# Data operations moved off GpSimd, and the modulation's accumulation ordered behind diag(1/rms), in a two-layer RWKV-7 / Hyena block on one core

## The chip, the cores and the metric

The kernel runs on one core of one Trainium2 chip. The metric is device time in microseconds (us): the median of 3 runs was 3515.73 (3511.09 to 3516.47). One further execution was taken by the hardware profiler; all rows shown are from it.

The engines are named as in the profile: PE (TensorE matmul), PEld (its weight load), DVE (VectorE), ACT (ScalarE), POOL (GpSimd), SP (SyncE, which here only issues DMAs). Each engine works through its own instructions in the order in which they stand, and waits on semaphores for the others. A DMA is issued by an instruction in the queue of SP or of POOL; if that instruction has to wait, what stands behind it in that queue waits too.

## The reference, cut to what matters

Two layers on a latent stream x of 256 tokens x 2048 channels, with a context of 256 tokens as prefix in the first layer. Layer 0 mixes tokens with a bidirectional RWKV-7 scan, layer 1 with a Hyena long convolution; each mixer is followed by a squared-ReLU MLP of width 8192.

```python
for i in range(DEPTH):                              # 2 layers
    mod = (silu_c @ ada_w[i] + ada_b[i]).reshape(B, N_MOD, 1, D)     # 2048 x 12288 per layer
    h = modulate(rms_norm(x, norm_g[i, 0]), mod[:, 0], mod[:, 1])
    y = rwkv_mixer(...) if kind == 0 else hyena_stream(h, ...)
    x = x + mod[:, 2] * rms_norm(y, norm_g[i, 1])
    h = modulate(rms_norm(x, norm_g[i, 2]), mod[:, 3], mod[:, 4])
    x = x + mod[:, 5] * rms_norm(squared_relu_mlp(h, mlp_up[i], mlp_down[i]), norm_g[i, 3])
```

Two parts of it matter here. The first is `mod`, the modulation: one row vector silu(c), 2048 long, times a 2048 x 12288 matrix per layer. It is a matrix-vector product, whose 100 MB of weights per layer have to be fetched. The second is `x + gate * rms_norm(y)`, the residual at the end of each of the four sublayers, with the next sublayer's norm right behind it.

In the mixer of layer 0, the decay and the in-context rate are sigmoids of low-rank products (two directions each, 2048 channels x 512 tokens), and the scan is done in chunks, for which triangular 32x32 systems are inverted.

## The kernel before, in words

**Stages.** In the order of time of the profiled execution: norms and modulation of layer 0 (to about 200 us); the RWKV projections (200 to 440); the beginning of the scan, in which the low-rank products and the first chunks overlap (440 to 520); the scan in groups of heads (520 to 1280); the Hyena filters and the rest of the scan (to 1386); the RWKV output gemm (1386 to 1470); first transition T1 (1470 to 1530); MLP of layer 0, `mlp0` (1530 to 2240); second transition T2 (2240 to 2285); Hyena's input gemm and convolutions (2285 to 2650); Hyena's output gemm (2650 to 2744); third transition T3 (2744 to 2797); MLP of layer 1, `mlp1` (2797 to 3495); the last residual. The transition's numbers run from the last matmul of a gemm to the first sublayer matmuls that run without a break.

**Gemms.** Each fp32 weight block `w` (128 x 1024, loaded by SP) is cut by ACT into a high part `wh` and by DVE into a low part `wl`, and three matmuls per block (`hxh,wh`; `hxl,wh`; `hxh,wl`) make the product. In mlp0 and mlp1 these keep PE busy without a pause.

**A transition** is `resid` (from L443) with `rstd` in it. The token-major outputs (tiles `o` or `y`) are squared by ACT with a row sum (`ysq`), DVE sums the four quarters into `ss`, ACT takes the square root, DVE the reciprocal, and two DVE instructions write `dg`, a 128x128 diagonal matrix of 1/rms for each half of the tokens (L463). Only then can PE go on: `sg` matmuls (L469) transpose the output and scale it in one product with `dg`. For each of 16 channel blocks DVE then makes x (residual), ACT the high part `hxh` of the next input and the squares `sq`, DVE the low part `hxl`, and PE the sums of squares (L423) and the next gemm's matmuls. When all 16 are there, `rstd` is computed (ACT square root, DVE reciprocal) and the first products of the next gemm are scaled by it (`nt` in an MLP, `z` in Hyena).

**The modulation** of what is needed later is computed beside other stages by `ada_run`, which is a generator: the surrounding code advances it by a step now and then (`bg`, `rate`). It works on sets: one set is 512 columns of `ada_w`. For a set, 16 blocks of 128 rows are loaded into tiles `aw`, two blocks per load (`per=2`, 512 KB) or one (`per=1`, 256 KB), in two buffers, and for each block DVE adds the block, scaled by a column `sc` of silu(c), to the sum `acc` (128x512): a TENSOR_SCALAR for the first block (L332), 15 SCALAR_TENSOR_TENSOR for the others (L334). Four small matmuls with a column of ones then sum over the partitions (L313). `ADA = (4, 8, 16, 8, 4)` gives the number of sets in the RWKV projections, the scan (there in another way, by PE), mlp0, Hyena and mlp1. A load into `aw` has to wait until the acc step that read this buffer is done. The loads of mlp0's sets (128 x 512 KB) and of the RWKV projections (64 x 256 KB) are in SP's queue, between the loads of the weights; those of Hyena (128 x 256 KB) and of mlp1 (32 x 512 KB) are in POOL's queue.

**What sets the order.** The instructions are emitted in program order into a scheduler that places them by a simulated time line and by priorities; `high_priority` (around `ss` to `dg`) draws instructions forward. The order on each engine is then fixed in the program, and so an acc step that stands ahead of the chain to `dg` on DVE is waited for, even where its load is late.

**POOL** does four other things: 32 of the 64 instructions t*0.5+0.5 behind the tanh of the low-rank products in `lora2` (L750, tile `l2t`; the other 32 are on DVE); in `scan_prepare`, for each of 8 groups, the memset of the 128x1024 tile W of the triangular inversion and of its diagonal (L1303 and L1304, printed as tile `d`); the memset of the two edge columns of each of 48 tiles `z` in Hyena (L1581); and the issue of the loads `fx` of the scan's projections (L857) with the stores `xv` and `xr` behind which they stand.

Of the kernel before, what the change touches and what calls it, by code (L numbers as in the profile page):

```python
# [10 lines left out]
F32 = mybir.dt.float32  # L11
F32R = mybir.dt.float32r
BF16 = mybir.dt.bfloat16
AF = mybir.ActivationFunctionType
# [4 lines left out]
P = 128  # L19
D = 2048  # L20
KT = D // P
L = 256
# [47 lines left out]
class Kern:  # L70
    def __init__(self, nc, tc, I, out, scr, upto=99):
        nc = Nc(self, nc)
        self.nc, self.tc, self.I, self.out, self.scr = nc, tc, I, out, scr
        self.bg, self.credit, self.rate = [], 0.0, 0.0
        self.upto = upto
        self.wraw, self.wsp = [], []

# [22 lines left out]
    def pin(self, key, r):  # L100

        if self.pins is not None and key in self.pinned:
            prev = self.pins.get(key)
            if prev is not None:
                self.tc.add_manual_dep(r.ins, prev.name, mybir.DependencyInfo(mybir.DependencyClass.NoSync, mybir.DependencyReason.DATA),
                                       reason="order of the scan")
            self.pins[key] = r.ins
        return r

# [130 lines left out]
    def setup(self, es):  # L240
# [17 lines left out]
        nc.vector.memset(self.ones, 1.0)  # L258
        self.eps = cst.tile([P, 2], F32, name="eps")
# [45 lines left out]
    def ada_run(self, n, pool, psum="mm", on_pool=True, per=2, bufs=2, behind=None, queue=None):  # L305
# [12 lines left out]
        for layer, ch, i in itertools.islice(self.ada_todo, n):  # L318
            acc = pool.tile([P, 512], F32, name="acc", bufs=per)
            c0 = ch * D + i * 512  # L320
            for k in range(0, KT, per):
# [3 lines left out]
                for a in range(per):  # L325
# [5 lines left out]
                    elif k + a == 0:  # L331
                        nc.vector.tensor_scalar(acc, w[:, a], s, None, op0=ALU.mult)  # L332
                    else:
                        nc.vector.scalar_tensor_tensor(acc, w[:, a], s, acc, op0=ALU.mult, op1=ALU.add)  # L334
# [108 lines left out]
    def resid(self, x, y, ss, layer, gi, ch, pool, nxt=None):  # L443
# [13 lines left out]
        with self.tc.high_priority(self.PRT):  # L457
# [4 lines left out]
            for tt in range(2):  # L462
                nc.vector.tensor_scalar(dg[:, tt], self.ident, ss[:, 1, tt : tt + 1], None, op0=ALU.mult)  # L463
# [242 lines left out]
    def lora2(self, pool):  # L706
# [33 lines left out]
        for q in range(4):  # L740
            for nm, e in (("dec", 0), ("dec", 1), ("a", 0), ("a", 1)):
                b0 = self.hw0 if nm == "dec" else self.ha0
                w = next(block)
                for j in range(4):
# [5 lines left out]
                    (nc.gpsimd if m % 4 < self.LPOOL else nc.vector).tensor_scalar(t, t, 0.5, 0.5, op0=ALU.mult, op1=ALU.add)  # L750
# [521 lines left out]
    def scan_prepare(self, g):  # L1272
# [30 lines left out]
        nc.gpsimd.memset(W, 0.0)  # L1303
        nc.gpsimd.memset(fl(W)[:, 0:1024:33], 1.0)  # L1304
# [251 lines left out]
    LPOOL = 2  # L1556
# [3 lines left out]
    def hyena(self, x, ada, nada):  # L1560
        nc, tc, I = self.nc, self.tc, self.I
        with ExitStack() as es:
# [7 lines left out]
            fp = pool("hf", 4)  # L1570
            r = self.xr
            ys = []
            self.bg, self.rate = [itertools.islice(ada, nada // 4)], nada / 4 / 11
            for dc in range(4):
                secs = []
                for s in range(3):
                    zc = [None] * 4

                    def ev(m, ps, s=s, zc=zc):
                        z = zp.tile([P, L + 2], F32, name="z", bufs=2)  # L1580
                        nc.gpsimd.memset(z[:, 0 : L + 2 : L + 1], 0.0)  # L1581
# [173 lines left out]
    def run(self):  # L1755
        nc, tc = self.nc, self.tc
        with ExitStack() as es:
# [28 lines left out]
            with ExitStack() as e1:  # L1786
# [7 lines left out]
                for i, phase in enumerate((lambda: self.mlp(x, 0), lambda: self.hyena(x, (), 0), lambda: self.mlp(x, 1))):  # L1794
                    if self.upto >= 3 + i:
                        with ExitStack() as e2:
                            if self.ADA[2 + i]:
                                ad = self.pool(e2, "ad")
                                per = 1 if i == 1 else 2
                                ada = self.ada_run(self.ADA[2 + i], ad, "sg", self.ONP[2 + i], per, queue=nc.gpsimd if i else None)  # L1800
# [98 lines left out]
```

## Time and profile before

The profiled execution took 3515.95 us, of which the trace's span covers 3513.1; 2.85 us lie around it. The profiled execution is 0.22 us above the median of the runs shown.

| | before |
|---|---|
| median of 3 runs | 3515.73 us (3511.09 to 3516.47) |
| profiled execution | 3515.95 us, span 3513.1 us |
| PE busy | 3290.9 us (94%) |
| DVE busy | 2474.5 us (70%) |
| ACT busy | 1638.0 us (47%) |
| POOL busy | 253.4 us (7%), 476 instructions |
| mean granted TensorE clock | 0.974 |

PE is the engine to read first: it works during 94% of the span, so a change can gain at most in the pauses of PE and in the stretches where its clock is low. A stage in which PE is busy all the time is not shortened by moving DVE's or POOL's work; a transition is, if what moves was in the chain that PE waits for.

### The profile page before, as it was taken

The page shows a single profiled execution, that of the slowest core. Times are in us where ns is not written, and L with a number is a line of the kernel's source. Part 1 is how long each engine was busy: PE and PEld are TensorE (multiplying, and loading weights), DVE is VectorE, ACT ScalarE, POOL GpSimd, SP SyncE. Part 2 cuts the span into 40 slices and gives each one's busy share as a digit, 9 for nine tenths or more (in the row PEclk, how much of TensorE's full clock was granted, in tenths as well). Part 3 has the DMA queues.
Part 4 walks back from the last instruction along what each step waited for, and adds up shares of the span by engine and source line. Part 5 has one row for each costly group of instructions (what it writes and reads, how often), then busy time and mean ns, then how long its engine had stood idle before and what let it go on. Part 6 is the DMA issues. An engine that isn't in the chain of part 4 may idle for free.

```text
span 3513.1 us, 74240 instructions
## 1 busy us (share of the span) xinstructions
PE 3290.9 (94%) x30598; PEld 2886.2 (82%) x30598; DVE 2474.5 (70%) x4059; ACT 1638.0 (47%) x2878; POOL 253.4 (7%) x476
## 2 busy tenths in 40 slices
PE   6799888989999888899999999999999899999999
PEld 3377677878888766798989899899997798989897
DVE  4798776767777755587777876588997875555554
ACT  4554454555444444444444444454453444444453
POOL 0011121111111000000000001011110100000000
PEclk9999999999999989999999999999999999999999
DMA  9668899989889745688888886477775775555653
GB/s 313 204 227 278 277 330 283 289 267 272 269 267 277 219 140 182 202 260 285 277 299 279 297 282 236 142 250 238 240 231 185 242 243 188 183 189 187 188 189 120
DMA packets 575515, 836.76 MB, mean 238 GB/s; under 512 B 39551, under 2 KB 373280, under 8 KB 575176
## 3 DMA queue, kind: packets, MB, share of 16 engines
q1 hardware_dynamic: 529224, 668.42, 59.3%
q0 software_dynamic: 45952, 163.60, 14.7%
q8 instruction: 239, 3.92, 0.5%
q14 instruction: 100, 0.82, 0.1%
HBM read 777.31 MB, written 54.59 MB: 237 GB/s over the span
## 4 chain that ended last, share of the span: by engine, by line
PE 60%; DMA 11%; DVE 8%; issue 5%; ACT 2%; SPq 1%; POOL 0%; DVEq 0%; POOLq 0%; ACTq 0%
PE mm L112 47%; DMA aw<-in_ada_w 4%; PE sg L112 4%; PE fl L112 4%; PE sc L112 3%; DVE tmp L53 1%; DVE d L53 1%; DVE wl L53 1%; DMA cum<-cum 1%; DMA fx<-xv 1%; DMA w<-in_hy_in_w 1%; DVE acc L53 1%; DMA win<-in_window 1%; DMA fr<-in_w_v 1%; PE sg L469 1%
## 5 line engine op out<-in xcount | busy, mean ns | idle before, releaser
L53 DVE TENSOR_TENSOR wl<-w,wh 128x1024 fp32r<-128x1024 f32 (+1 forms) x716 | 871.2, 1219 | 394.7 <-ACT wh L53 394.4
L53 ACT CAST wh<-w 128x1024 fp32r<-128x1024 f32 (+1 forms) x716 | 747.0, 1046 | 774.5 <-PE mm L112 677.7
L112 PE MATMUL mm<-hxh,wh 128*128 128x258 f32 x2816 | 798.2, 285 | 3.6 <-DVE nt L53 3.6
L112 PE MATMUL mm<-hxl,wh 128*128 128x258 f32 x2816 | 797.9, 284 | 0.0
L112 PE MATMUL mm<-hxh,wl 128*128 128x258 f32 x2816 | 797.3, 284 | 0.0
L112 PEld LDWEIGHTS mm<-hxh,wh 128*128 128x128 f32 x2816 | 532.0, 189 | 5.2 <-issue 3.7
L112 PEld LDWEIGHTS mm<-hxl,wh 128*128 128x128 f32 x2816 | 534.0, 190 | 1.7
L112 PEld LDWEIGHTS mm<-hxh,wl 128*128 128x128 f32 x2816 | 531.2, 189 | 1.4
L53 DVE SCALAR_TENSOR_TENSOR acc<-aw,sc,acc 128x512 f32<-128x512 f32 x480 | 358.8, 748 | 156.6 <-DMA aw<-in_ada_w 153.6
L112 PE MATMUL mm<-wh,uh 128*128 128x512 f32 x1024 | 403.0, 394 | 0.0
L112 PE MATMUL mm<-wh,ul 128*128 128x512 f32 x1024 | 401.0, 392 | 0.0
L112 PE MATMUL mm<-wl,uh 128*128 128x512 f32 x1024 | 398.5, 389 | 0.0
L112 PEld LDWEIGHTS mm<-wh,ul 128*128 128x128 f32 x1024 | 192.2, 188 | 43.9
L112 PEld LDWEIGHTS mm<-wl,uh 128*128 128x128 f32 x1024 | 192.3, 188 | 41.8
L112 PEld LDWEIGHTS mm<-wh,uh 128*128 128x128 f32 x1024 | 192.3, 188 | 39.4
L112 PE MATMUL fl<-fh,fx 128*128 128x256 f32 x1024 | 213.4, 296 | 9.7 <-DMA fx<-xv 8.7
L324 POOL DMA_DIRECT2D aw<-in_ada_w x160 | 91.6, 573 | 1464.2 <-ACT uh L53 954.6
L112 PEld LDWEIGHTS fl<-fh,fx 128*128 128x128 f32 x1024 | 168.4, 194 | 27.6 <-issue 13.8
L112 PE MATMUL fl<-flo,fx 128*128 128x256 f32 x512 | 146.3, 286 | 0.1
L112 PE MATMUL sg<-ard,KB 64*64 64x64 f32 (+1 forms) x3584 | 128.5, 244 | 11.8 <-DVE NT L53 3.7
L53 DVE TENSOR_TENSOR flo<-fr,fh 128x512 fp32r<-128x512 f32 x128 | 88.3, 690 | 66.3 <-ACT fh L53 53.0
L112 PE MATMUL mm<-xl,wh 128*128 128x512 f32 (+1 forms) x288 | 116.1, 403 | 11.4 <-DVE xl L53 11.4
(359 smaller groups left out, 5712.5 us busy)
## 6 DMA issues: line engine op xcount, KB each, us to landing
aw<-in_ada_w SPq DMA_DIRECT2D x256, 512.0 KB, 6.0
w<-in_mlp_down SPq DMA_DIRECT2D x128, 1024.0 KB, 5.3
w<-in_mlp_up SPq DMA_DIRECT2D x120, 1024.0 KB, 6.5
fx<-xv POOLq DMA_DIRECT2D x128, 512.0 KB, 6.3
w<-in_hy_in_w SPq DMA_DIRECT2D x44, 1024.0 KB, 6.3
fx<-xr POOLq DMA_DIRECT2D x64, 512.0 KB, 5.7
aw<-in_ada_w POOLq DMA_DIRECT2D x128, 256.0 KB, 4.1
w<-in_w_k SPq DMA_DIRECT2D x16, 1024.0 KB, 7.3
```

Source lines behind the costliest of these rows:

```text
L53: return self.kern.pin(self.key, f(*a, **kw))
L112: return self.pin("pe", self.nc.tensor.matmul(out, lhsT=lhsT, rhs=rhs, **kw))
L324: (queue or nc.sync).dma_start(w, self.I["ada_w"][layer, k * P : (k + per) * P, c0 : c0 + 512].rearrange("(a p) n -> p a n", p=P))
L469: nc.tensor.matmul(pt[:, s], lhsT=y[k // 4, tt][:, k % 4 * P : (k % 4 + 1) * P], rhs=dg[:, tt], start=True, stop=True)
```

## The change

Five edits in one kernel.

1. `resid` remembers its last `dg` instruction (`self.end`), and `follow` adds an ordering from it to each acc instruction of `ada_run` that is emitted later, with no semaphore. On DVE these acc steps thus stand behind the `dg` of the sublayer that was emitted last before them.
2. The 32 `l2t` operations of POOL become ACT activations (Identity, scale 0.5, bias from a new 128x1 tile `half`).
3. The memsets of W go from POOL to DVE.
4. Hyena's 48 `z` tiles become two fixed tiles used in turn, whose edge columns are set to zero once, by DVE.
5. The loads of mlp0's sets go from SP's queue to POOL's.

After it, POOL's queue holds DMA issues alone.

```diff
+        self.end = None                       # Kern.__init__
...
+    def follow(self, r):
+        if self.end is not None:
+            self.tc.add_manual_dep(r.ins, self.end.name, mybir.DependencyInfo(mybir.DependencyClass.NoSync, mybir.DependencyReason.DATA),
+                                   reason="order at the end of a stage")
...
+        self.half = cst.tile([P, 1], F32, name="half")
+        nc.vector.memset(self.half, 0.5)
...
                     elif k + a == 0:
-                        nc.vector.tensor_scalar(acc, w[:, a], s, None, op0=ALU.mult)
+                        self.follow(nc.vector.tensor_scalar(acc, w[:, a], s, None, op0=ALU.mult))
                     else:
-                        nc.vector.scalar_tensor_tensor(acc, w[:, a], s, acc, op0=ALU.mult, op1=ALU.add)
+                        self.follow(nc.vector.scalar_tensor_tensor(acc, w[:, a], s, acc, op0=ALU.mult, op1=ALU.add))
...
-                nc.vector.tensor_scalar(dg[:, tt], self.ident, ss[:, 1, tt : tt + 1], None, op0=ALU.mult)
+                self.end = nc.vector.tensor_scalar(dg[:, tt], self.ident, ss[:, 1, tt : tt + 1], None, op0=ALU.mult).ins
...
-                    (nc.gpsimd if m % 4 < self.LPOOL else nc.vector).tensor_scalar(t, t, 0.5, 0.5, op0=ALU.mult, op1=ALU.add)
+                    if m % 4 < 2:
+                        nc.scalar.activation(t, t, AF.Identity, scale=0.5, bias=self.half)
+                    else:
+                        nc.vector.tensor_scalar(t, t, 0.5, 0.5, op0=ALU.mult, op1=ALU.add)
...
-        nc.gpsimd.memset(W, 0.0)
-        nc.gpsimd.memset(fl(W)[:, 0:1024:33], 1.0)
+        nc.vector.memset(W, 0.0)
+        nc.vector.memset(fl(W)[:, 0:1024:33], 1.0)
...
+            zs = [c1.tile([P, L + 2], F32, name=f"z{i}") for i in range(2)]
+            for z in zs:
+                nc.vector.memset(z[:, 0 : L + 2 : L + 1], 0.0)
...
-                        z = zp.tile([P, L + 2], F32, name="z", bufs=2)
-                        nc.gpsimd.memset(z[:, 0 : L + 2 : L + 1], 0.0)
+                        z = zs[m % 2]
...
-                                ada = self.ada_run(self.ADA[2 + i], ad, "sg", self.ONP[2 + i], per, queue=nc.gpsimd if i else None)
+                                ada = self.ada_run(self.ADA[2 + i], ad, "sg", self.ONP[2 + i], per, queue=nc.gpsimd)
```

What the ordering moves is not seen in the diff. In T1, on DVE, the rows around `dg` before (`o` is the gemm's output, `wl` the low part of mlp0's weights):

```order
L53 TENSOR_TENSOR ss<-ss 128x2
L53 TENSOR_SCALAR acc<-aw,sc_92 128x512
L53 TENSOR_TENSOR wl<-w,wh 128x1024
L53 RECIPROCAL ss<-ss 128x2
L53 SCALAR_TENSOR_TENSOR acc<-aw,sc_92,acc 128x512
L53 TENSOR_SCALAR dg<-ident,ss 128x128 x2
L53 SCALAR_TENSOR_TENSOR acc<-aw,sc_92,acc 128x512 x2
```

In the changed kernel the rows there are `ss`, `wl`, RECIPROCAL, `dg` x2, and then TENSOR_SCALAR `acc`: two acc steps went from in front of `dg` to behind it, and `wl` stayed where it was. In T2, on DVE, with Hyena's first set, the changed kernel has

```order
L53 TENSOR_TENSOR ss<-ss 128x2
L53 RECIPROCAL ss<-ss 128x2
L53 TENSOR_SCALAR dg<-ident,ss 128x128 x2
L53 TENSOR_SCALAR acc<-aw,sc_94 128x512
L53 SCALAR_TENSOR_TENSOR acc<-aw,sc_94,acc 128x512
L53 SCALAR_TENSOR_TENSOR x<-sg,gg,x 128x256 x2
L53 SCALAR_TENSOR_TENSOR hxl<-x,gs,hxh 128x256
L53 SCALAR_TENSOR_TENSOR acc<-aw,sc_94,acc 128x512
L53 SCALAR_TENSOR_TENSOR x<-sg,gg,x 128x256
L53 SCALAR_TENSOR_TENSOR hxl<-x,gs,hxh 128x256
L53 SCALAR_TENSOR_TENSOR acc<-aw,sc_94,acc 128x512
```

where before there were only x and `hxl` from `dg` on. All 16 acc steps of the set now stand between `dg` and the reciprocal of `rstd`; before they stood in the last part of mlp0. In T3, on DVE, the rows before were

```order
L53 TENSOR_TENSOR y<-mm,ob 128x512
L53 TENSOR_TENSOR wl<-w,wh 128x1024
L53 SCALAR_TENSOR_TENSOR acc<-aw,sc_92,acc 128x512
L53 TENSOR_TENSOR ss<-ss 128x2
L53 SCALAR_TENSOR_TENSOR acc<-aw,sc_92,acc 128x512
L53 RECIPROCAL ss<-ss 128x2
L53 SCALAR_TENSOR_TENSOR acc<-aw,sc_92,acc 128x512
L53 TENSOR_SCALAR dg<-ident,ss 128x128 x2
L53 TENSOR_TENSOR wl<-w,wh 128x1024
```

and are now, with mlp1's weights `wl` still among them,

```order
L53 TENSOR_TENSOR y<-mm,ob 128x512
L53 TENSOR_TENSOR ss<-ss 128x2
L53 TENSOR_TENSOR wl<-w,wh 128x1024
L53 RECIPROCAL ss<-ss 128x2
L53 TENSOR_SCALAR dg<-ident,ss 128x128 x2
L53 TENSOR_SCALAR acc<-aw,sc_94 128x512
L53 SCALAR_TENSOR_TENSOR acc<-aw,sc_94,acc 128x512 x2
L53 SCALAR_TENSOR_TENSOR x<-sg,gg,x 128x256 x2
```

The acc steps of mlp1's first two sets, of which 26 stood ahead of `dg` between the weights of Hyena's output gemm and 9 between `dg` and the reciprocal of `rstd`, are all behind `dg` now: 23 of them ahead of that reciprocal, the others after it. In T1 the number between `dg` and that reciprocal goes from 22 to 24. `sc_92` and `sc_94` are the same tile of silu(c).

More of the change, by code (lines that the diff above doesn't have):

```diff
@@ L1555 @@
     PRB = 200
-    LPOOL = 2
     FX = 3
```

## The prediction

> **What bounds the kernel now.** I read the page's engine rows and chain first, then the windows by stage, then PE's pauses in the timeline.
>
> ```profile
> span 3513.1 us, 74240 instructions
> PE 3290.9 (94%) x30598; PEld 2886.2 (82%) x30598; DVE 2474.5 (70%) x4059; ACT 1638.0 (47%) x2878; POOL 253.4 (7%) x476
> PE 60%; DMA 11%; DVE 8%; issue 5%; ACT 2%; SPq 1%; POOL 0%; DVEq 0%; POOLq 0%; ACTq 0%
> ```
>
> PE bounds: it is busy for 94% of the span and has 60% of the chain that ended last. POOL has 0% of that chain. So the 253.4 us of POOL are not on offer; what can be gained or lost are PE's pauses, 3513.1 - 3290.9 = 222 us. The windows (columns: length, then busy time of PE, PEld, DVE, ACT, POOL, granted clock, DMA share, GB/s) say where they lie:
>
> ```profile
> 440.00:520.00 80.00, 67.88 (x526) 59.53 (x525) 57.71 (x105) 43.86 (x88) 23.05 (x32) 0.94 1.03 335
> 520.00:1280.00 760.00, 680.21 (x13888) 595.41 (x13887) 539.88 (x1175) 371.91 (x878) 96.08 (x181) 0.94 0.85 258
> 1530.00:2240.00 710.00, 709.01 (x4523) 645.54 (x4521) 537.64 (x731) 314.12 (x446) 9.82 (x20) 1.00 0.82 271
> 2285.00:2650.00 365.00, 363.27 (x2776) 350.73 (x2775) 325.83 (x516) 184.99 (x294) 63.89 (x155) 1.00 0.74 239
> 2650.00:2755.00 105.00, 87.57 (x402) 69.80 (x401) 74.59 (x105) 38.20 (x55) 10.22 (x15) 0.94 0.63 208
> 2797.00:3495.00 698.00, 698.00 (x4430) 634.81 (x4429) 398.59 (x496) 310.73 (x445) 8.53 (x12) 1.00 0.59 190
> ```
>
> mlp0 (1530 to 2240), Hyena's main part (2285 to 2650) and mlp1 (2797 to 3495) leave PE idle for 1.0, 1.7 and 0 us: nothing that moves inside them shows. The pauses that this change touches are those in front of the transitions and, in T1, inside one. The PE timeline gives the first `sg` matmul of T1, T2 and T3 with its pause in brackets, and T1's pause at the `nt` products:
>
> ```profile
> 1478.30 1.01 PE L469 MATMUL sg<-dg,o 128*128 128x128 f32 x3 [8.75 <-DVE dg L53]
> 1526.94 0.36 PE L112 MATMUL mm<-hxh,wh 128*128 128x258 f32 x1 [3.64 <-DVE nt L53]
> 2242.37 0.60 PE L469 MATMUL sg<-dg,o 128*128 128x128 f32 x3 [3.36 <-DVE dg L53]
> 2754.70 0.58 PE L469 MATMUL sg<-dg,y 128*128 128x128 f32 x1 [10.58 <-DVE dg L53]
> ```
>
> **The change, term by term.** The ordering works in two directions: acc steps leave the chain to `dg`, and come back between `dg` and the reciprocal of `rstd`, for which PE waits next.
>
> *T1 ahead of dg.* DVE there:
>
> ```profile
> 1475.70 0.48 DVE L53 TENSOR_SCALAR acc<-aw,sc 128x512 f32<-128x512 f32 x1 [1.58 <-DMA aw<-in_ada_w]
> 1476.10 1.22 DVE L53 TENSOR_TENSOR wl<-w,wh 128x1024 fp32r<-128x1024 f32 x1
> 1477.24 0.15 DVE L53 RECIPROCAL ss<-ss 128x2 f32<-128x2 f32 x1
> 1477.31 0.73 DVE L53 SCALAR_TENSOR_TENSOR acc<-aw,sc,acc 128x512 f32<-128x512 f32 x1
> 1477.96 0.47 DVE L53 TENSOR_SCALAR dg<-ident,ss 128x128 f32<-128x128 f32 x2
> ```
>
> The first acc holds DVE until 1476.10 (its load is late by 1.58), the second from 1477.31 to 1477.96. In the new order `wl` stays ahead of the reciprocal; it can then start at about 1475.5 instead of 1476.10, and `dg` follows the reciprocal at once: 0.6 + 0.65 = 1.2 us off the pause of 8.75. Bounds: 0.65 (`wl` is held by ACT's `wh` in any case) and 2.1 (0.65 with all of the 1477.24 - 1475.8 that `wl` takes). I take -1.2.
>
> *T3 ahead of dg.* DVE there, after the output gemm's last matmul at 2744.1 (2754.70 - 10.58):
>
> ```profile
> 2744.33 1.53 DVE L53 SCALAR_TENSOR_TENSOR acc<-aw,sc,acc 128x512 f32<-128x512 f32 x2
> 2749.52 0.68 DVE L53 TENSOR_TENSOR y<-mm,ob 128x512 f32<-128x512 f32 x1
> 2752.14 0.74 DVE L53 SCALAR_TENSOR_TENSOR acc<-aw,sc,acc 128x512 f32<-128x512 f32 x1
> 2752.91 0.75 DVE L53 SCALAR_TENSOR_TENSOR acc<-aw,sc,acc 128x512 f32<-128x512 f32 x1
> 2753.58 0.16 DVE L53 RECIPROCAL ss<-ss 128x2 f32<-128x2 f32 x1
> 2753.70 0.75 DVE L53 SCALAR_TENSOR_TENSOR acc<-aw,sc,acc 128x512 f32<-128x512 f32 x1
> 2754.37 0.47 DVE L53 TENSOR_SCALAR dg<-ident,ss 128x128 f32<-128x128 f32 x2
> ```
>
> The three acc steps from 2752.14 on cost 0.66 + 0.2 (the square root runs beside the second) + 0.67 = 1.5 us: the least gain. The two at 2744.33 and others delay the eviction of `y`; if all of it goes, T3's pause becomes T1's without its acc, 8.75 - 1.2 = 7.55, a gain of 3.0. Since the stretch is also fed by late weights, more would need an earlier gemm end. I take -3, bounds -1.5 and -4.
>
> *Behind dg, in all three.* The windows from the first `sg` to the end of `rstd`, same columns:
>
> ```profile
> 1478.00:1527.00 49.00, 42.04 (x297) 39.67 (x297) 39.24 (x68) 21.49 (x45) 0.00 (x0) 0.95 0.72 223
> 2242.30:2282.00 39.70, 39.27 (x290) 38.10 (x291) 24.56 (x44) 21.72 (x44) 0.00 (x0) 0.96 0.39 122
> 2754.60:2795.00 40.40, 39.92 (x290) 38.40 (x291) 31.42 (x56) 20.94 (x43) 4.26 (x6) 0.94 0.65 200
> ```
>
> T2 and T3 take 39.7 and 40.4 us, with PE at 99%: PE paces them. T1 does the same work in 49, with DVE busy for 39.24, that is 80%. It carries 22 acc steps ahead of the reciprocal, T3 nine, T2 none. What T1 waits for is in the tile view of acc (first its operations, then DVE's idle time ahead of them):
>
> ```profile
> L53 DVE SCALAR_TENSOR_TENSOR acc<-aw,sc,acc x24: 651/744/753, 1477.3 to 1527.4; 128x512 f32<-128x512 f32 x24
>   DMA aw<-in_ada_w: 8.8, 6
> ```
>
> An acc step costs 0.66 to 0.74 us of DVE, and with two buffers the next load is asked for only when a step is done: 8.8 us of DVE's waiting in T1 are for `aw`, with x and `hxl` queued behind, and PE behind these.
>
> In the new order T2 has 16 of them and T3 23. T2's DVE work becomes 24.56 + 16 x 0.7 = 35.8 us. It still fits 39.7 if no load is late (0, PE paces); at T1's share it needs 35.8 / 0.80 = 44.7 (+5.0). I take +3, since its 16 steps are the second part of 8 turns of two 256 KB loads, which have to follow one another in 40 us. A load that comes 1 us late more often gives the upper end, +8. T3's DVE work becomes 31.42 + 14 x 0.7 = 41.2, over the 40.4 by itself (+0.8); at T1's share 51.5 (+11). I take +5, a little under the middle, because the nine steps there now leave no pause behind `dg`. T1 gets two steps more, 1.4 us of DVE of which PE's own pace hides some: +1 (0 to 1.4). In T1 the loads also change queues. By landing:
>
> ```profile
> aw<-in_ada_w SPq DMA_DIRECT2D x256, 512.0 KB, 6.0
> aw<-in_ada_w POOLq DMA_DIRECT2D x32, 512.0 KB, 5.4
> ```
>
> From POOL they land 0.6 us sooner, but in quieter stages, and POOL's issue takes time by itself (0.573 below). I take 0, bounds -2 and +4: some six turns in T1 at 0.6 us each way. In mlp0 itself the other loads have PE's 709 of 710 us as cover; without it 128 x 0.573 = 73 us of POOL would still run beside DVE.
>
> *What leaves POOL.* Its groups, and the rows that price the replacements:
>
> ```profile
> L324 POOL DMA_DIRECT2D aw<-in_ada_w x160 | 91.6, 573 | 1464.2 <-ACT uh L53 954.6 <-DVE acc L53 438.6 <-PE sc L112 30.0
> L750 POOL TENSOR_SCALAR l2t<-l2t 128x512 f32<-128x512 f32 x32 | 32.1, 1009 | 43.2 <-ACT l2t L53 40.8 <-DMA raw<-in_dec_w 1.4 <-DMA a<-l2t 0.7
> L1303 POOL MEMSET d<- 128x1024 f32 x8 | 7.8, 971 | 0.0
> L53 ACT ACTIVATE ysq<-o 128x512 f32<-128x512 f32 x24 | 15.1, 631 | 44.3 <-DVE o L53 44.2
> L53 DVE MEMSET wide<- 128x512 f32 x2 | 1.0, 485 | 0.1
> 793.91 0.69 DVE L53 TENSOR_TENSOR flo<-fr,fh 128x512 fp32r<-128x512 f32 x1 [1.54 <-ACT fh L53]
> ```
>
> The 32 `l2t` cost ACT 32 x 0.63 = 20 us in place of 32.1 on POOL. They are spread over the projections and 440 to 520, where ACT is busy for 43.86 of 80 us and PE idle for 12. If a quarter stands there (an assumption), ACT gets 5 us, and the loads `fx` no longer stand behind a waiting `l2t`. Either may win: 0, bounds -4 and +4. The memsets of W put 2 x 0.485 + 0.07 = 1.04 us on DVE per group, 8.3 in all, right behind the transpose of the group. DVE idles soon after (1.54 us ahead of `flo` in the group shown; 220 of the scan's 760 us in all), so a part is absorbed: +1, bounds 0 and +8.3 (no cover). The z tiles lie in a stage where PE has 363.27 of 365: 0, bounds -1 and +1.
>
> *Sum.* T1 -1.2 + 1, T2 +3, T3 -3 + 5, W +1, the rest 0: +5.8 us on the profiled 3515.95, so 3521.75, and by the median (0.22 lower) **3521.5**.
>
> [...]
>
> **The rivals.**
>
> A (forecast): pauses ahead of `dg` shrink by 4 us, acc steps behind `dg` give back more. 3512 to 3530.
>
> B (faster): PE goes on pacing T2 and T3, since 35.8 and 41.2 us of DVE nearly fit 40 and PE's matmuls of the next gemm fill the waits. Then T1 -1.2, T3 -4, T1's loads -2, the freed `fx` -4: -11, 3505. For it: T3 with nine acc steps shows no pause behind `dg`. Against: T1 at 80% DVE does.
>
> C (slower): each acc in T2 and T3 waits for its load as in T1. T2 +8, T3 +11 - 1.5, T1 +4, and W uncovered +4 more: +25, 3541; its place is the DVE queue behind `dg`, and it decides from the point where T2's first `z` comes later than the 2281.7 of now (row below), since PE has no other product ready then. A milder form, T2 +5, T3 +11 - 3, W +1, gives 3529.
>
> D (POOL's issue stretched): one and the same operation of POOL varies much in the tile view of `l2t` (min, median and max in ns):
>
> ```profile
> L750 POOL TENSOR_SCALAR l2t<-l2t x32: 609/762/2734, 223.5 to 480.7; 128x512 f32<-128x512 f32 x32
> ```
>
> Should whatever stretches it by up to 2.1 us stretch POOL's issues too, six turns in T1 and six in T3 are 12 x 2.1 = 25 us later on top of A: 3546; at the mean stretch, 1009 - 609 = 400 ns, 5 us: 3526. The mean of 573 ns of `aw` speaks against it. [...]
>
> E (nothing happens): the scheduler's `wl` still hold the chain to `dg`, and loads land early enough: 3516.
>
> **How the numbers follow.** A 0.42, B 0.22, C 0.22, D 0.03, E 0.11. The bounds of the single terms add to far more than would fall together; the range 3505 to 3534 holds A, E, the milder C and most of B. The likeliest one's own range is 3512 to 3530. This kernel's measurement can tell about 0.2%, 7 us: faster is below 3508.7, slower above 3522.8. From the cases: faster 0.22 (B and a tip of A, less B's weak part); slower 0.39 (C, D and 0.14 of A); same 0.39.
>
> **What would show it.** In the changed profile: T1's pause 7.5 instead of 8.75; T3's 7 to 9 instead of 10.58; T2's unchanged at about 3.4. DVE waits for `aw` inside T2 and T3, and PE pauses with releaser `nt`, `z` or x that were not there: 3 and 5 us. In T2 the first `z`,
>
> ```profile
> 2281.74 0.42 DVE L53 TENSOR_TENSOR z<-mm,rstd 128x256 f32<-128x256 f32 x1
> ```
>
> now 39.4 us behind the first `sg`, would stand at 42 to 45. POOL's list has `aw`, `fx`, `xv`, `xr` alone. If T2 and T3 keep 40 us each, I am wrong and B holds; if the scan's 760 us grow by over 4, W had no cover; if the stretch 440 to 520 changes by more than 4, I misjudged `l2t`.

## The result and the profile after

The changed kernel takes 3534.49 us (median of 7 runs, 3529.06 to 3544.91), the kernel before 3515.73 (3503.63 to 3523.57, 7 runs). The ratio is 1.0063, 95% interval 1.0047 to 1.0080: slower by about 22 us (17 to 28). The forecast was 3521.5 with a range to 3534. The sign of the likeliest case was right, its size was not, and the time lies just outside the range.

The profiled execution of the changed kernel is the one of 3534.49 us. Its page, then its windows over the three stretches from the first `sg` to the first `z` or `nt` (columns as in the prediction):

```profile
span 3532.1 us, 74071 instructions
PE 3302.4 (93%) x30598; PEld 2896.8 (82%) x30598; DVE 2474.6 (70%) x4078; ACT 1656.5 (47%) x2910; POOL 297.4 (8%) x508
PE 60%; DMA 13%; issue 11%; DVE 11%; ACT 3%; SPq 0%; POOL 0%; DVEq 0%; ACTq 0%; POOLq 0%
```

```profile
1489.60:1538.00 48.40, 43.64 (x296) 41.53 (x296) 39.66 (x68) 21.50 (x44) 8.54 (x12) 0.89 0.73 225
2252.10:2300.70 48.60, 42.47 (x296) 40.05 (x296) 36.17 (x64) 22.95 (x47) 8.60 (x16) 0.92 0.63 198
2768.90:2814.00 45.10, 41.34 (x296) 39.20 (x297) 39.49 (x69) 21.12 (x45) 8.52 (x12) 0.95 0.75 238
```

DVE is as busy as before (2474.6 us against 2474.5), and still the chain that ended last has more DVE and DMA in it (11% and 13% against 8% and 11%). T2 went from 39 to 48 us and T3 from 40 to 45; T1 stayed at 48. The PE timeline shows the pauses:

```profile
1489.64 0.58 PE L478 MATMUL sg<-dg,o 128*128 128x128 f32 x1 [10.27 <-DVE dg L53]
2252.17 0.58 PE L478 MATMUL sg<-dg,o 128*128 128x128 f32 x1 [3.36 <-DVE dg L53]
2300.76 0.55 PE L119 MATMUL mm<-hxh,wh 128*128 128x258 f32 x1 [4.08 <-DVE z L53]
2768.97 0.58 PE L478 MATMUL sg<-dg,y 128*128 128x128 f32 x1 [6.69 <-DVE dg L53]
2814.02 0.55 PE L119 MATMUL mm<-hxh,wh 128*128 128x258 f32 x1 [3.23 <-DVE nt L53]
```

T3's pause ahead of `dg` fell from 10.58 to 6.69, as forecast, but T1's rose from 8.75 to 10.27, and two pauses of 4.08 and 3.23 us are new behind T2's and T3's chains.

To place the rest, one takes the same events out of each trace and compares the lengths between them. The table gives the length of each stretch before, and by how much it differs in four other traces (us). "Changed, again" is a second profile of the same program; "order" and "order + queue" are the first and fourth experiment below.

```
stretch                                    before  changed  changed,again  order  order+queue
start to end of RWKV projections            433.0     +4.4       +6.1       +1.3      +1.3
... to last scan matmul                     919.7     +1.2       -1.6       +0.2      +3.6
... to last output-gemm matmul              116.9     +4.3       -0.2       +0.7      +0.1
... to first sg (T1's pause)                  8.8     +1.5       +1.4       -1.7      +1.4
... to first nt                              48.1     -0.1       +0.1       -3.2      +1.7
... to end of mlp0, T2's pause included     716.0     -1.5       +0.9       -1.5      +0.4
T2: first sg to first z                      39.4     +8.7       +8.6       +8.0      +8.0
... to Hyena's output gemm                  331.7     +2.7       +0.8       +2.4      +2.2
Hyena's output gemm                         130.7     -3.0       -3.4       -3.1      -4.1
T3's pause                                   10.6     -3.9       -3.3       -3.9      -4.0
T3: first sg to first nt                     39.7     +4.8       +4.4       +6.3      +5.4
... to end                                  718.8     -0.1       +2.1       +2.3      -0.4
```

The transitions repeat from trace to trace within a microsecond or so. The long stretches ahead of T1 do not: two profiles of one program differ by 2 to 5 us there, so a difference in them means something only over several profiles.

### The profile page after: what moved, and what is told of

Read it like the earlier page. It is cut to its first block, busy times and chain, and to the rows that moved or that the text cites. A ratio compares the mean times of both kernels' runs of the same rounds, so it can differ in the third digit from the quotient of the medians.

```text
span 3532.1 us, 74071 instructions
## 1 busy us (share of the span) xinstructions
PE 3302.4 (93%) x30598; PEld 2896.8 (82%) x30598; DVE 2474.6 (70%) x4078; ACT 1656.5 (47%) x2910; POOL 297.4 (8%) x508
## 4 chain that ended last, share of the span: by engine, by line
PE 60%; DMA 13%; issue 11%; DVE 11%; ACT 3%; SPq 0%; POOL 0%; DVEq 0%; ACTq 0%; POOLq 0%
PE mm L119 44%; DMA aw<-in_ada_w 6%; PE sg L119 5%; PE fl L119 5%; PE sc L119 4%; DVE wl L53 1%; DVE d L53 1%; DVE tmp L53 1%; DVE acc L53 1%; DMA cum<-cum 1%; DMA fr<-in_w_v 1%; DMA win<-in_window 1%; DVE xt L53 1%; DVE flo L53 1%; DMA a<-a 1%
## 5 line engine op out<-in xcount | busy, mean ns | idle before, releaser
L333 POOL DMA_DIRECT2D aw<-in_ada_w x288 | 182.6, 634 | 1517.6 <-DVE acc L53 1073.5
L119 PEld LDWEIGHTS mm<-wl,uh 128*128 128x128 f32 x1024 | 192.4, 188 | 41.6
L119 PEld LDWEIGHTS sg<-ard,KB 64*64 64x64 f32 x3584 | 110.4, 136 | 19.7 <-DVE NT L53 4.7
```

What stands on the lines that cost most here:

```text
L119: return self.pin("pe", self.nc.tensor.matmul(out, lhsT=lhsT, rhs=rhs, **kw))
L333: (queue or nc.sync).dma_start(w, self.I["ada_w"][layer, k * P : (k + per) * P, c0 : c0 + 512].rearrange("(a p) n -> p a n", p=P))
```

## The experiments

Each run was timed against the kernel before on the same chip. A ratio of 1.001 is 3.5 us.

**The parts one at a time.** First the ordering alone:

```diff
+    self.follow(nc.vector.scalar_tensor_tensor(acc, ...))   # and end = dg, in the kernel before
```

> The kernel before with the ordering behind dg alone (loads of mlp0 stay in SP's queue, POOL keeps its data operations). Theory M (acc steps behind dg hold DVE, PE pauses in T2 and T3 and its clock falls after each pause of over 3 us): +8 to +14 us, PE pauses of 3 to 5 us at the reciprocal of rstd in T2 and T3, T3's pause ahead of dg down from 10.6 to about 7. Rival Q (the queue move is what costs): within 4 us of before.

Measured: 1.0015 (0.9999 to 1.0032), +5 us. T2 took 8.0 us more, T3's pause fell by 3.9, T3 itself rose by 6.3. That is less than the 8 to 14 of the theory. The pauses of PE that it foresaw behind T2's and T3's chains are there (3.6 and 3.9 us), but in this profile T1 gained, its pause 1.7 and its length 3.2. What it says of the clock is counted here on the profiles of the kernel before and of the changed kernel: 16 pauses of PE of 3.1 us and more began at full clock, and in the 5 us behind each the mean granted clock was 0.50 to 0.66. Behind two pauses of 3.00 us it was 0.66 (before, from 1208.8) and 1.00 (changed, from 1211.3).

Then the queue alone:

```diff
-    queue=nc.gpsimd if i else None
+    queue=nc.gpsimd
```

> The kernel before with only mlp0's loads moved from SP's queue to POOL's. Theory M: within 4 us of before, T2 and T3 as before. Rival Q: the weights of the MLP land later in T1 because they now share the DMA engines with loads that no longer take turns with them in one queue; T1's pause ahead of dg grows to 10 us or more and the time rises by 5 to 10 us.

Measured: 1.0001 (0.9985 to 1.0016). The time is as theory M has it, but T1's pause is as Q has it: it grew to 11.83 us. So the queue move does make T1's pause longer; in the whole time, which this run gives to about 5 us, it does not show.

Then POOL's three data operations:

```diff
-    nc.gpsimd.memset(W, 0.0)      # l2t of m % 4 < 2 to nc.scalar.activation, z static
+    nc.vector.memset(W, 0.0)
```

> The kernel before with only the three edits that take data operations from POOL (l2t to ACT, memset of W to DVE, two fixed z tiles). Theory M: +1 to +6 us (the projections ended 3 us later in the changed kernel, the scan no later). Rival S (the spread of small operations to ACT and DVE is what costs): +10 us or more.

Measured: 1.0016 (0.9996 to 1.0036), +6 us. Inside the expectation of theory M, though the interval touches zero.

The ordering and the queue together:

> The ordering and the queue move together, POOL's data operations as before. Theory M with parts that add: the sum of the two single runs, +8 to +16 us. Rival: the two only cost together (T1's steps and loads both change place), so this run is slower than the sum of the singles by over 5 us.

Measured: 1.0032 (1.0017 to 1.0047), +11 us, against 5.3 + 0.4 for the two singles. The intervals are too wide to call the surplus of some 5 us proven.

The changed kernel with the loads of mlp0 back on SP:

> The changed kernel with mlp0's loads back in SP's queue. Theory Q2 (with the loads on POOL the weights that stand in front of the reciprocal in T1 land late, and only then): T1's pause ahead of dg goes from 10.3 to about 7, T1's first nt from 48 us behind the first sg to about 45, and the time is some 6 us under the changed kernel, 10 to 12 over before (the two singles are +5.3 and +5.6). Rival: the time stays within 3 us of the changed kernel, the queue costs nothing here either.

Measured: 1.0057 (1.0038 to 1.0075), +20 us. T1's pause became 7.1 us, as Q2 says, but the whole fell by only about 2 us against the changed kernel's 1.0063. The rival is nearer. T1's length stayed at 48.5 us, where 45 was expected. Beside the ordering alone (+5) POOL's three edits cost some 15 us here, not 6.

**The two edits on POOL's operations.** The `l2t` edit alone:

> The kernel before with only the l2t operations moved from POOL to ACT. Theory L (ACT evicts the PSUM of the projections, and its longer queue holds PE): the projections end 4 to 5 us later, the whole is 3 to 6 us slower. Rival W (the memset on DVE is what costs in the three-edit run): projections as before, whole within 2 us of before.

Measured: 1.0009 (0.9997 to 1.0020); the projections ended 0.6 us earlier, not 4 to 5 later. By this trace alone theory L falls, though the time, +3 us, is inside its 3 to 6. Then the memsets of W alone:

> The kernel before with only the memsets of W moved from POOL to DVE. Theory W (what costs in the three-edit run, +5.6, is these memsets, as l2t alone was +3 with an interval over zero): +2 to +6 us, the scan longer by as much. Rival (their cover on DVE holds): within 2 us of before, and the three edits' price is l2t and the rest is below what can be told.

Measured: 1.0012 (0.9998 to 1.0027), +4 us, as theory W has it, the scan longer by 8.5 in its profile. One pair of traces tells nothing for stretches that vary by 5 us, so I took all twenty profiles of this study together. Those with `l2t` on ACT (8) reach the end of the projections at 436.3 us on average, those without (12) at 433.4: +2.9 with a standard error of 1.0. From the first to the last scan matmul, the 8 with the memsets on DVE take 903.8 us, the 12 others 898.0: +5.8 with a standard error of 2.1. Seven of the 8 traces are the same in both counts, so the averages alone do not part the two edits; what parts them is the place (the first memset of W comes after the end of the projections) and, with one trace each, the scan of 897.1 us with `l2t` alone and of 911.0 with the memsets alone. The scan also varies widely without either edit, from 889.8 to 904.9 us.

By this count both edits cost, together 9 us; the timed run of all three has 6. Three more pairs of timed runs differ by POOL's three edits alone: the changed kernel with mlp0's loads on SP against the ordering alone (+15), the changed kernel against ordering and queue (+11), and two runs shown further down, the changed kernel with Hyena's sets freed against the order for the MLP sets with the queue move (+14). With the +6 the four average 11 us, each good to 7 to 9. Which wait carries it was not found: in both stretches it is spread over many small ones.

**The place to stand behind.** The acc steps ordered behind the reciprocal of `rstd` instead of `dg`, so that none stands in a transition:

```diff
-    self.end = nc.vector.tensor_scalar(dg[:, tt], ...).ins
+    self.end = nc.vector.reciprocal(r[:, :n], r[:, :n]).ins     # in rstd, when called from resid
```

> The kernel before with the acc steps ordered behind the reciprocal of rstd of each transition instead of behind dg; queues and POOL as before. Theory M (what costs in the order alone is the acc steps between dg and rstd): T1, T2 and T3 each take 39 to 41 us from the first sg to the first nt or z (48, 39 and 40 before; 45, 47 and 46 with the order behind dg), T3's pause ahead of dg stays near 6.7, and the whole is 10 to 18 us faster than before. Rival B (PE is held by something else there, the weights or the clock): the transitions stay over 43 us and the time is within 5 us of before.

Measured: 1.0103 (1.0086 to 1.0121), 36 us slower. Theory M was right on the transitions and wrong on the time: T1 fell from 48.1 to 37.6 us, T2 stayed at 39.1, T3 went to 38.2. The steps were only pushed further, and came due all at once. PE's pauses in mlp0 and at the end of Hyena's stage:

```profile
1644.86 0.51 PE L119 MATMUL mm<-wl,uh 128*128 128x512 f32 x1 [2.24 <-DVE wl L53]
1671.71 0.79 PE L119 MATMUL mm<-wl,uh 128*128 128x512 f32 x1 [2.52 <-DVE wl L53]
2648.83 0.34 PE L320 MATMUL sg<-ones,acc 128*128 128x2 f32 x1 [7.12 <-DVE acc L53]
2677.42 0.51 PE L119 MATMUL sc<-uh,dftch 128*128 128x512 f32 x1 [4.28 <-DVE pa L53]
```

mlp0 took 13 us more, and Hyena's output gemm with what overlaps it 32 more. Hyena has 128 loads to work off before its stage ends, so what it does not do early, it does late.

**Late loads or DVE's work?** In the changed kernel, Hyena's first set is made from two loaded blocks only:

```diff
+    if queue and per == 1 and last is None and k > 1:
+        w = kept[k % 2]            # no load, no wait; 16 steps as before
```

> The changed kernel, in which Hyena's first set loads only its first two blocks and uses these two in turn for all 16 steps: 14 loads of 256 KB and the waits for them are left out (so that set's modulation is not computed), the 16 DVE steps stay. Theory A (late loads hold the chain): T2 from 48 us to 39.5 to 41.5, no pause of 3 us ahead of the first z, time 6 to 10 us under the changed kernel. Rival D (the 11 us of DVE work itself holds the chain): T2 stays at 45 us or more.

Measured: T2 41.6 us from the first `sg` to the first `z` (39.4 before, 48.0 changed). DVE's rows for acc in T2, of the changed kernel:

```profile
L53 DVE SCALAR_TENSOR_TENSOR acc<-aw,sc,acc x15: 741/751/752, 2252.7 to 2287.5; 128x512 f32<-128x512 f32 x15
  DMA aw<-in_ada_w: 6.8, 7
```

Without the loads the same view has 15 steps of 747 ns and no wait. Its window, to be compared with the changed kernel's T2 above:

```profile
2252.10:2294.20 42.10, 41.00 (x296) 39.65 (x297) 35.85 (x63) 23.03 (x47) 1.07 (x2) 0.93 0.45 141
```

DVE does the same 36 us of work in a window of 42.1 us, to the first products behind `z`, that took 48.6 with the waits. So of T2's +8.7, 6.4 go with the loads that were left out, 4.9 of them ahead of the last x, and 2.2 stay with DVE's work. The run takes away the traffic of these loads together with the waits for them, and the two are not told apart: the transform table `dft`, which ACT cuts in T2 as well, landed 3.4 us after its issue instead of 6.3. The time was 1.0021 (1.0005 to 1.0037), 7 us over before and 12 to 15 under the changed kernel's two runs, more than the 6 to 10 expected.

A third buffer for Hyena's loads, nothing left out:

```diff
-    ada_run(..., per, queue=nc.gpsimd)
+    ada_run(..., per, 3 if i == 1 else 2, queue=nc.gpsimd)
```

> The changed kernel with three buffers instead of two for the loads of Hyena's sets (256 KB each). Theory A (late loads): T2 from the first sg to the first z goes from 48 to 42 to 45 us, the pause of 4 us ahead of the first products' scaling shrinks under 2, time 3 to 8 us under the changed kernel. Rival D (DVE's own work): T2 stays within 1.5 us of 48.

Measured: T2 44.0 us, the length that theory A gave, but only in small part by its way. The acc steps still waited 5.1 us for `aw` in T2 (6.8 in the changed kernel), and the last x came 35.5 us behind the first `sg` instead of 36.4. The other 3 us of the gain lie behind the last x: the set's last acc step began 25.5 us behind the first `sg` instead of 35.3, and after that the weight that ACT had waited 2.54 us for needed no wait, and the table `dft` landed after 3.2 us instead of 6.3. The time was 1.0061 (1.0042 to 1.0080), as the changed kernel and not 3 to 8 us under it: Hyena's output gemm took 10 us more than before and T3 8 more. A shorter transition did not by itself make the kernel faster.

**Where the order costs.** The order for the sets of the MLPs alone (T1 and T3), and then for Hyena's alone (T2):

```diff
+    follow = self.follow if per == 2 else lambda r: r      # i1: per == 1
```

> The kernel before with the order behind dg for the sets of the two MLPs alone; Hyena's sets may stand ahead of T2's dg as before. Theory M2 (the order costs in T2 and what follows it, and gains or evens out in T1 and T3): the order alone was +5.3, of which T2 and Hyena's stage carry 10.4 in its profile, so -5 us (-9 to -1). Rival G (T1's gain comes back later as it did with the order behind rstd): within 2 us of before. T2 from the first sg to the first z 39 to 40 us.

> The kernel before with the order behind dg for Hyena's sets alone, which touches T2 only. Theory M2: T2 47 to 48 us, T1 and T3 as before, whole +7 to +12 us; with the order for the MLP sets alone (-1.5) it adds up to the order for all (+5.3) to within 4. Rival: under +4 us, the loss needs the order in all three places.

Measured: 0.9996 (0.9980 to 1.0011) for T1 and T3, -1 us where -5 was expected; 1.0043 (1.0027 to 1.0058), +15 us where 7 to 12 were expected, for T2, which took 49.6 us. The PE timeline of the second at T2's end:

```profile
2280.85 0.55 PE L119 MATMUL mm<-hxh,wh 128*128 128x258 f32 x1 [4.82 <-DVE z L53]
```

T2 carries the loss of the order. The gain forecast for T1 and T3 did not come to more than could be told, and the sum of both (+14) is over the +5 of the order in all places by more than expected; the intervals of the three runs leave room for it.

The changed kernel with Hyena's sets freed from the order:

> The changed kernel with Hyena's sets freed from the order, all else as changed. Theory M2: 8 to 12 us under the changed kernel, +10 to +14 over before, T2 39 to 41 us. Rival: the parts only move, under 4 us below the changed kernel.

Measured: 1.0037 (1.0022 to 1.0053), +13 us, 7 to 9 under the changed kernel's two runs; T2 40.6 us. About as M2 says.

The changed kernel a second time:

> The changed kernel once more, for a second profile and beside the others on this chip. If the stage table of one profile is repeatable: T2 8 to 9 us longer than before, the first sg of T1 10 us behind the output gemm, T3's pause 6.7; the projections and the stretch from the filters to T1, which no single edit explains, should show how far two profiles of one kernel differ (3 to 5 us).

Measured: 1.0056 (1.0034 to 1.0077), and the table above.

The order for the MLP sets with the queue move:

> The order for the MLP sets alone, with mlp0's loads on POOL's queue. Theory Q3 (with the order in T1 the loads go out beside the last weights, and the weights ahead of the reciprocal land late): T1's pause 10 to 10.5 instead of 7.4, whole 3 to 7 us over the same kernel with the loads on SP, whose ratio was 0.9996. Rival: T1's pause as with SP, whole within 2 us of it.

Measured: T1's pause 11.02 us instead of 7.39, but the time 0.9998 (0.9984 to 1.0011), the same as on SP. The pause is the queue's, the time does not follow it here.

With this run four pairs differ by the order for Hyena's sets alone: T2's order alone (+15), the order in all places against the one for the MLP sets (+7), the changed kernel against the one with Hyena's sets freed (+9), and order and queue together against this run (+12). They average 11 us, each good to 5 to 8. T2's order and POOL's three edits thus cost about the same, and together they come to what the changed kernel lost.

**More buffers, for a better kernel.** Three and four buffers for the MLP sets' loads, with the order at T1 and T3, and four without any order:

```diff
+    ada_run(..., per, 2 if i == 1 else 4, queue=...)      # h2: 3
```

> The order for the MLP sets alone, with three buffers for their loads. Theory A: T1 from 46 to 42 us and T3 from 45 to 41 us, time 5 to 10 us under before. Rival N (the transfers share the DMA engines with the weights, so earlier asking only makes these late): T1 and T3 within 1.5 us of 46 and 45, the same time as with two buffers.

> The same with four buffers. Theory A: T1 and T3 at 40 to 42 us, time 8 to 14 us under before, no acc step in T1 or T3 waits for a load more than 2 us in sum. Rival N: as with three buffers, or worse, as weights land later ahead of dg in T1.

> The kernel before with four buffers for the MLP sets' loads, without the order. Theory A: T1 from 48 to 41 to 43 us, T3 unchanged at 40, T1's and T3's pauses ahead of dg unchanged (8.8 and 10.6 to within 1.5): 4 to 8 us under before. If the order matters beside the loads, the run with order and four buffers is 3 to 6 us below this one.

Measured: 0.9994 (0.9977 to 1.0011), 0.9993 (0.9981 to 1.0005) and 0.9989 (0.9974 to 1.0004). With the order, T1 and T3 hardly moved (46.7 and 44.8 us with three buffers, 46.6 and 44.5 with four). In T1 with four buffers DVE has 31 acc steps in place of 25, and waits 3.1 us for their loads in place of 7.2: the loads come sooner and more steps are put there. Without the order T1 did fall, to 42.2 us, and T3's pause ahead of `dg`, expected unchanged, fell to 5.1 us, less than with the order, behind an output gemm 4.6 us longer than before. All three are at most slightly faster than before, none by more than its interval; the last, four buffers and no order, has the lowest ratio and the lowest median of the study (3503.66 us against 3510.79). The change as a whole is beaten by the kernel before.

## Why the prediction was wrong, step by step

The sum was +5.8 us and should have been about 22. Two steps failed: T2's term, +3 where T2 and Hyena's stage lost 10.9, and the terms of POOL's operations, +1 and 0 where 5.8 and 2.9 were measured. T1, put at -0.2, lost 2.0 through the queue, and T3, put at +2, came out even.

**T1 ahead of dg (-1.2).** The mechanism was right: over six traces with an order and SP's queue the pause is 7.0 to 7.4 us, over five without order 8.3 to 8.9, a gain of 1.45. But the step took the queue move as neutral there, and with the loads on POOL the pause is 10.2 to 11.2 (seven traces). ACT and DVE in the changed kernel show what took the place of the acc steps:

```profile
1486.89 1.04 ACT L53 CAST wh<-w 128x1024 fp32r<-128x1024 f32 x1 [2.64 <-DMA w<-in_mlp_up]
1487.84 0.29 ACT L53 ACTIVATE ss<-ss,eps 128x2 f32<-128x2 f32 x1
```

```profile
1484.27 0.16 DVE L53 TENSOR_TENSOR ss<-ss 128x2 f32<-128x2 f32 x1 [0.85 <-ACT ysq L53]
1487.96 1.23 DVE L53 TENSOR_TENSOR wl<-w,wh 128x1024 fp32r<-128x1024 f32 x1 [3.53 <-ACT wh L53]
1489.11 0.15 DVE L53 RECIPROCAL ss<-ss 128x2 f32<-128x2 f32 x1
```

`ss` was ready at 1484.4, but the square root stands on ACT behind the cast of one more weight of mlp0, and the reciprocal on DVE behind its low part. Before, ACT waited 0.49 us for the weight in this place, and now 2.64; ACT in T1 before:

```profile
1474.42 1.04 ACT L53 CAST wh<-w 128x1024 fp32r<-128x1024 f32 x1 [0.49 <-DMA w<-in_mlp_up]
1475.37 0.29 ACT L53 ACTIVATE ss<-ss,eps 128x2 f32<-128x2 f32 x1
```

In the changed kernel POOL's queue issues its two `aw` loads while SP issues the weights:

```profile
1476.05 0.72 POOL L333 DMA_DIRECT2D aw<-in_ada_w  x1 [282.38 <-PE mm L119]
1479.36 0.73 POOL L333 DMA_DIRECT2D aw<-in_ada_w  x1 [2.60 <-DMA w<-in_mlp_up]
```

In SP's queue these two stood behind the weight: it was asked for at 1470.39, they at 1470.81. Now they are asked for 3.9 and 0.6 us ahead of the weight (SP issues it at 1479.97), and share the DMA engines with it: from its issue to its landing POOL's queue had 36% of the 16 engines' time beside the 60% of SP's, where before POOL's had none. The weight then took 6.8 us from issue to landing, and 4.0 before. The same weight took 7.25 us in the queue move alone and in the order for the MLP sets with it, and 3.6 with that order on SP's queue. So the queue move makes it late; that the sharing is how is inferred, since no run changed the order of these transfers alone. The prediction had named the wait (rival E: "the scheduler's `wl` still hold the chain to `dg`"), and had not connected it with the queue. It gave the queue move 0 with bounds of -2 and +4; at T1's pause it is +3.4, in the time between 0 and +6 (four comparisons).

**T3 ahead of dg (-3).** Right: -3.9 us over fifteen traces (6.8 against 10.7), and the output gemm ahead of it 2.7 shorter.

**Behind dg in T3 (+5).** Right: 44.7 us against 39.7, +5.0. With 1.9 more in mlp1 behind it, T3 comes out even (-2.7 - 3.9 + 5.0 + 1.9), where the prediction had +2.

**Behind dg in T2 (+3).** This is the first of the two steps that failed. The sum of DVE's work was good (35.8 forecast, 36.17 measured), and the two ends of the range were 0 and +8. DVE was busy for 74% of T2's window (36.17 of 48.60 us); the prediction had +5.0 at T1's 80%, and took less than that. What I took between them was too low, and the whole cost lies above the upper end: +8.9 in T2 (six traces against eleven), and another +2 until T3, the net of +4.0 in Hyena's main part and -2.0 in its output gemm. Nearly all of T2's part lies ahead of the last x, which came 36.4 us behind the first `sg` instead of 28.4: the acc steps' work stands in x's way, and so do their 6.8 us of waiting for loads, as in T1. From the last x to the first `z` it took 11.7 us instead of 11.0, although the instructions there changed places. DVE there before, then in the changed kernel, and ACT in the changed kernel:

```profile
2277.21 1.75 DVE L53 RECIPROCAL rstd<-rstd 128x256 f32<-128x256 f32 x1
2280.53 0.68 DVE L53 TENSOR_TENSOR dftcl<-dft,dftch 128x512 fp32r<-128x512 f32 x1
```

```profile
2296.10 0.69 DVE L53 TENSOR_TENSOR dftcl<-dft,dftch 128x512 fp32r<-128x512 f32 x1 [0.46 <-ACT dftch L53]
2296.85 0.69 DVE L53 TENSOR_TENSOR dftsl<-dft,dftsh 128x512 fp32r<-128x512 f32 x1
2297.46 1.75 DVE L53 RECIPROCAL rstd<-rstd 128x256 f32<-128x256 f32 x1
```

```profile
2293.34 1.05 ACT L53 CAST wh<-w 128x1024 fp32r<-128x1024 f32 x1 [2.54 <-DMA w<-in_hy_in_w]
2295.45 0.62 ACT L53 CAST dftch<-dft 128x512 fp32r<-128x512 f32 x1 [1.07 <-DMA dft<-in_dftc]
2296.20 0.62 ACT L53 CAST dftsh<-dft 128x512 fp32r<-128x512 f32 x1
2296.72 0.47 ACT L53 ACTIVATE rstd<-sc,eps 128x256 f32<-128x256 f32 x1
```

The scheduler put the preparation of Hyena's transform tables ahead of `rstd`, on ACT and on DVE; before, the reciprocal stood ahead of `dftcl` by 3.3 us. The reciprocal thus comes 8.9 us behind the last x instead of 6.5, but 1.8 of these 2.4 us come back, as the first `z` follows it after 2.7 us instead of 4.5: the tables stood ahead of that `z` in both kernels. With three buffers, where they stand ahead of `rstd` too, the reciprocal came 5.8 us behind the last x. So their new place costs little; what lengthens the stretch are the 2.54 and 1.07 us that ACT waits for a weight and a table. Why these two land late was not found: the table took 6.3 us in the changed kernel and 3.2 with three buffers, but 6.7 in the order for the MLP sets, where no `aw` load is near.

**The pause's second price.** The prediction counted a pause of PE at its length. The granted clock is the sixth figure behind the length. Ahead of T2's new pause, from 2258.0 to 2296.6, it was 1.00. Here it is in the 5 us from 2300.00, in which T2's new pause ends, in the changed kernel, and below it around the first `z` before:

```profile
2300.00:2305.00 5.00, 4.24 (x20) 4.28 (x21) 5.00 (x11) 3.08 (x7) 1.08 (x2) 0.50 0.74 240
2281.00:2286.00 5.00, 5.00 (x44) 5.00 (x44) 3.65 (x8) 2.97 (x8) 0.54 (x1) 1.00 0.73 235
```

By an estimate from these rows (half the clock for 5 us; 20 matmuls against 44), that costs some 2.5 us of PE. This is part of Hyena's +4.0; the rest of it was not resolved.

**W's memsets (+1) and l2t (0).** Both were put at or near the end without cost, because idle time lay nearby: 220 us of it on DVE in the scan, 36 of 80 on ACT at its beginning. Measured +5.8 and +2.9 over twenty profiles; the bounds, 8.3 and 4, held, and the four pairs of timed runs give 11 us for all three edits. This is the other step that failed. An `l2t` took 0.72 us on ACT, not 0.63, which is 3 us of work in all and explains little. Idle time of an engine in a window was no cover here. That the moved instructions stand in a chain which runs through these windows is the likely reason; it was not shown, as the wait was not found.

**The sum.** T1's pause +2.0 and its length 0, T2 with Hyena's stage +10.9, T3 +0.3, the scan +5.8, the projections +2.9: 22 us. That this is the measured ratio's 22 (17 to 28) is in part luck. The terms are averages over different sets of traces, and the shortening of Hyena's output gemm is counted twice, at -2.0 and at -2.7, where the two profiles of the changed kernel have 3.0 and 3.4 in all; counted once the sum is 23 to 24. No rival had this: B fell, since T2 and T3 do not keep 40 us; the mild form of C (3529) had T2 6 us too low and T3 8 us too high; D has no sign, for POOL's `aw` issues and landings are in the changed kernel:

```profile
L333 POOL DMA_DIRECT2D aw<-in_ada_w x288 | 182.6, 634 | 1517.6 <-DVE acc L53 1073.5
...
aw<-in_ada_w POOLq DMA_DIRECT2D x160, 512.0 KB, 5.6
```

An issue is 61 ns longer on average than before, with more of the larger loads among them.

## What to carry to other kernels

Taking work out of a chain is worth its price only where it can go to a place with slack; here the steps belong ahead of T2, in the tail of mlp0, where PE has 709 of 710 us of work to cover them, and the order took them out of just that place. When an order is changed, read the whole new neighbourhood of the instruction that is waited for, on each engine in its chain, and look for what else now stands ahead of it: in T1 a weight cast whose load came late held the chain longer than the work that had been moved away. Then ask whether the new neighbour stood ahead of the chain's end before as well, as the tables in T2 did. And price a queue by when its transfers go out beside others, not only by how long they take to land: here `aw` took 5.4 us from POOL's queue and 6.0 from SP's before the change, and the weight beside it took 6.8 instead of 4.0.

## What the runs showed that was not expected

Pauses of PE of 2.15 to 2.52 us were followed by a lower granted clock in two places and by the full clock in two others. Windows right behind a pause of 2.23 us in the changed kernel (T1, at 1520.69) and of 2.52 us in the run with the order behind `rstd`, in the kernel before, behind one of 2.15 us, and with four buffers and no order, behind one of 2.23 us:

```profile
1520.70:1524.70 4.00, 4.00 (x18) 3.76 (x19) 4.00 (x7) 2.54 (x5) 0.70 (x1) 0.61 0.92 291
```

```profile
1671.70:1675.70 4.00, 3.98 (x9) 3.13 (x10) 3.80 (x5) 1.99 (x2) 0.00 (x0) 0.50 0.70 201
```

```profile
1511.40:1515.40 4.00, 3.99 (x29) 3.78 (x30) 4.00 (x8) 1.63 (x4) 0.00 (x0) 1.00 0.73 206
```

```profile
1525.30:1530.00 4.70, 4.66 (x39) 4.69 (x40) 4.70 (x10) 2.34 (x7) 0.00 (x0) 1.00 0.59 169
```

The clock fell to 0.61 and 0.50 behind the first two and stayed at 1.00 behind the other two, one of which was as long as the first. At these lengths the length alone does not tell which pause a lower clock follows; behind the 16 pauses of 3.1 us and more that were counted it was always lower. And two profiles of one and the same program differed by up to 5 us in the stretches ahead of T1. In the 12 traces without the memsets on DVE the scan ranged over 15 us, more than the 8.5 us by which the one trace with these memsets alone was longer than before.
